# Rotating 96 images by 90 degrees: ten of twelve slabs turned in pairs, and one slab stored in the middle of the loads

## The chip, the cores and the metric

The kernel runs on one core of one Trainium2 chip. The metric is the device time of one execution in microseconds (us), as the median of several runs; lower is better.

## The reference

```python
def setup_inputs():
    batch, c, h, w = 32, 3, 256, 256
    return {"x": np.random.randn(batch, c, h, w).astype(np.float32)}

def reference(x):
    return np.rot90(x, k=-1, axes=(-2, -1)).astype(np.float32)
```

Each of the 96 planes of 256 x 256 floats is turned clockwise: `out[i, j] = x[255 - j, i]`. Nothing is computed; 25.17 MB are read, permuted and 25.17 MB are written.

## The kernel before

**Slabs.** The 96 planes are cut into twelve slabs of eight planes, 2 MB each. A slab lies in SBUF as 128 partitions of 4096 floats (16 KB). A slab can be laid out in two ways, and the way decides how long the contiguous piece of DRAM is that one partition holds, and so how long a DMA row (one contiguous piece) is:

- "short": the slab is two halves of four planes, and a partition holds 8 image rows (8 KB) of each half. The DRAM rows are 8 KB, all 128 partitions take part.
- "long": a partition holds 16 image rows (16 KB) of one plane. The first four planes sit in the even partitions, the other four in the odd ones. The DRAM rows are 16 KB, and one half of a slab takes 64 partitions.

**Turning.** VectorE's 32 x 32 block transpose with a permuted access pattern does the whole rotation of a slab between two SBUF layouts. It can't go from long to long within one slab: a slab that is loaded long is stored short, and the reverse. Two slabs held side by side in one tile can be turned together from long to long, as one operation in four parts. So there are three forms in `turn`:

- slabs 0, 1 and 2 (`long_st`) are loaded short and stored long, two instructions each;
- slabs 3 to 7 are loaded long and stored short, two instructions each;
- the pairs (8, 9) and (10, 11) (`both`) are loaded long and stored long, four instructions a pair.

**Memory.** All twelve slabs fill SBUF, so each turn writes into the buffer of a slab that was turned before. The first one, slab 0, is turned into PSUM (`turned0`); at the end ScalarE copies it from PSUM into the buffer of slab 11, which is free by then, and it is stored from there. `home` and `pairs` say which buffer a turned slab goes to. The tile for slabs 3 and 7 is one pool tile for two slabs, as those of (8, 9) and (10, 11); the program waits per tile, not per slab.

**Order.** All DMAs are issued by SyncE (SP) on one queue. The order is: all loads (slabs 0, 1, 2, 3, 7, 4, 5, 6, 8 to 11); then the stores of slabs 4, 3, 5, 6, 7 (8 KB rows), 1, 2 (16 KB rows); then the pairs (8, 9) and (10, 11), each after its turn; then slab 0. The first store waits by hand for a piece of the last load: the first half of slab 11 is cut for that into a piece of 14 image rows (`mark`) and one of two. Every DMA uses one of eight completion semaphores in turn, so SP waits before a DMA until the one eight places ahead of it has landed.

**Lines.** L92, L88 and L96 issue the loads, L118 is the transpose, L124, L127 and L130 issue 16 KB row stores (L124: both halves of a slab in one DMA of 2 MB), L132 issues 8 KB row stores, L146 is the copy out of PSUM.

Of the kernel before, what the change touches and what calls it, by code (L numbers as in the profile page):

```python
# [1 line left out]

# [4 lines left out]

@with_exitstack
def kernel(
    ctx: ExitStack,
    tc: tile.TileContext,
    x: bass.AP,
    out: bass.AP,
):

    nc = tc.nc
    fp32 = mybir.dt.float32

    B, C, H, W = x.shape
    P = nc.NUM_PARTITIONS
    RL, RS = 16, 8  # L50
    I = 2
    Q = P * RS // H
    n_slabs = B * C // (Q * I)
    last = n_slabs - 1
    F = RS * W
    long_st = (0, 1, 2)
    both = (8, 10)
    paired = [n + a for n in both for a in range(2)]

    rows_in = x.rearrange("b c h w -> (b c h) w")  # L60
    rows_out = out.rearrange("b c h w -> (b c h) w")

    def short(rows):
        return rows.rearrange("(n i p r) w -> n p i (r w)", i=I, p=P, r=RS)

    def long(rows):
        return rows.rearrange("(n i m r) w -> n i m (r w)", i=I, m=P // I, r=RL)

    ld_short, ld_long, st_short, st_long = short(rows_in), long(rows_in), short(rows_out), long(rows_out)

    units = [None] * n_slabs
    adjacent = [(3, 7), (8, 9), (10, 11)]
    pairs = []
    for us in adjacent + [(u,) for u in range(n_slabs) if all(u not in us for us in adjacent)]:
        pool = ctx.enter_context(tc.tile_pool(name=f"unit{us[0]}", bufs=1))
        held = pool.tile([P, len(us), I * F], fp32, name=f"u{us[0]}")
        for j, u in enumerate(us):
            units[u] = held[:, j]
        pairs.append(held)
    psum = ctx.enter_context(tc.tile_pool(name="psum", bufs=1, space=bass.MemoryType.PSUM))  # L80
    turned0 = psum.tile([P, I * F], fp32, name="turned0")

    def fours(t):
        return t.rearrange("p (i f) -> p i f", i=I)

    for n in (0, 1, 2, 3, 7, 4, 5, 6, *range(8, n_slabs)):
        if n in (1, 2):
            nc.sync.dma_start(out=fours(units[n]), in_=ld_short[n])  # L88
            continue
        for i in range(I):  # L90
            if n in long_st:
                ld = nc.sync.dma_start(out=fours(units[n])[:, i], in_=ld_short[n][:, i])  # L92
            else:
                cuts = (0, 14 * W, RL * W) if (n, i) == (last, 0) else (0, RL * W)
                for f0, f1 in zip(cuts, cuts[1:]):
                    ld = nc.sync.dma_start(out=units[n][i::I, f0:f1], in_=ld_long[n, i][:, f0:f1])  # L96
                    if f1 == 14 * W:
                        mark = ld

    home = [turned0] + units[:last]  # L100

    def turn(n):
        if n in long_st:
            src = fours(units[n]).rearrange("p i (r g c) -> p c r g i", r=RS, c=RL)
            dst = home[n].rearrange("p (c k r) -> p c r k", c=RL, r=RS)[:, :, ::-1, ::-1]
            parts, step = 2, RL // 2
        elif n in paired:
            if n not in both:
                return
            src = pairs[both.index(n) + 1].rearrange("p a (r g c) -> p c r g a", r=RL, c=RL)  # L110
            dst = pairs[both.index(n)].rearrange("p i (c k r) -> p c r k i", c=RL, r=RL)[:, :, ::-1, ::-1, :]
            parts, step = 4, RL // 4
        else:
            src = units[n].rearrange("p (r g c) -> p c r g", r=RL, c=RS)
            dst = fours(home[n]).rearrange("p i (c k r) -> p c r k i", c=RS, r=RL)[:, :, ::-1, ::-1, :]
            parts, step = 2, RS // 2
        for h in range(parts):
            nc.vector.transpose(out=dst[:, h * step : (h + 1) * step], in_=src[:, h * step : (h + 1) * step])  # L118

    def store(n):  # L120
        if n in paired:
            first = n if n in both else n - 1
            if n == first:
                nc.sync.dma_start(out=st_long[n].transpose([1, 0, 2]), in_=pairs[both.index(n)][::I])  # L124
                return
            for i in range(I):
                nc.sync.dma_start(out=st_long[n, i], in_=pairs[both.index(first)][n - first :: I, i])  # L127
        elif n in long_st:
            for i in range(I):
                nc.sync.dma_start(out=st_long[n, i], in_=home[n][i::I])  # L130
        else:
            return nc.sync.dma_start(out=st_short[n], in_=fours(home[n]))  # L132

    for n in range(both[0]):
        turn(n)
    for n in (4, 3, 5, 6, 7, 1, 2):
        st = store(n)
        if n == 4:
            tc.add_manual_dep(st.ins, mark.ins.name, mybir.DependencyInfo(
                mybir.DependencyClass.Sync, mybir.DependencyReason.SCHED_ONLY), reason="stores after loads")  # L140
    for n in range(both[0], n_slabs):
        turn(n)
        store(n)

    for i in range(I):
        nc.scalar.copy(out=fours(units[last])[:, i], in_=fours(turned0)[:, i])  # L146
    home[0] = units[last]
    store(0)


# [1 line left out]
_INS = ['x']  # L152
_OUTS = [((32, 3, 256, 256), 'float32')]


# [23 lines left out]
```

## Time and profile before

| | |
|---|---|
| time, median of 3 runs | 123.2 us (123.16 to 123.3) |
| span of the profiled execution | 121.4 us |
| moved | 25.17 MB read, 25.17 MB written, 414 GB/s over the span |
| busy share of the 16 DMA engines | 98.0% |
| VectorE busy | 90.5 us (75%), 24 instructions |
| ScalarE busy | 4.9 us (4%) |
| DMAs | 23 loads and 17 stores, all on one queue |

The time is taken outside the profile. For the profiled execution only its span is on record, from the first to the last profiled instruction; the median lies 1.8 us above it, for what a launch does before and after. In the page, the row DMA gives the busy share of the DMA engines in 40 slices of the span in tenths, and the row GB/s what they moved in each slice. A mark L118 is line 118 of the kernel. In the list of waits of SP, a name on the left is the line whose instruction waited.

### The profile page before, as it was taken

To read this page: it belongs to the slowest core of one execution; us is meant where nothing else is said; L and a number is where in the kernel's file an instruction comes from. 1 tells how busy PE (TensorE), PEld (TensorE's weight loads), DVE (VectorE), ACT (ScalarE), POOL (GpSimd) and SP (SyncE) were. 2 spreads that over 40 slices of the span, in tenths; PEclk is the share of its full clock that TensorE was granted. 3 is DMA by queue.
4 is the path that set the end of the run, shared out by engine and by line. 5 is a ranking of instruction groups with operands and counts; after the bars stand their busy time and mean duration, and the time that the engine had idled before them with its cause. 6 is when DMAs were issued, how large, how long until landed. Compare 5 with 4: busy or idle time off the path is not lost.

```text
span 121.4 us, 134 instructions
## 1 busy us (share of the span) xinstructions
DVE 90.5 (75%) x24; ACT 4.9 (4%) x3; POOL 0.2 (0%) x4
## 2 busy tenths in 40 slices
DVE  0029999999999999999999999999999960000000
ACT  0000000000000000000040000000000038000000
POOL 0000000000000000000000000000000000000000
DMA  3999999999999999999999999999999999999994
GB/s 84 416 432 424 426 459 432 432 432 426 426 432 426 416 421 432 421 426 450 403 424 426 426 429 429 421 432 424 464 426 432 432 432 432 432 432 432 432 432 178
DMA packets 4800, 50.33 MB, mean 414 GB/s; under 512 B 640, under 2 KB 640, under 8 KB 704
## 3 DMA queue, kind: packets, MB, share of 16 engines
q1 hardware_dynamic: 4800, 50.33, 98.0%
HBM read 25.17 MB, written 25.17 MB: 414 GB/s over the span
## 4 chain that ended last, share of the span: by engine, by line
DVE 55%; issue 17%; DMA 6%; DVEq 3%; ACT 2%; ACTq 1%; SPq 0%
DVE u L118 50%; DVE turned L118 6%; DMA u<-in_x_dram 6%; DVEq L174 3%; ACT u L146 2%; ACTq L174 1%; SPq L92 0%; DVEq L118 0%
## 5 line engine op out<-in xcount | busy, mean ns | idle before, releaser
L118 DVE STREAM_TRANSPOSE u<-u 128x2048 f32<-128x2048 f32 x22 | 83.4, 3861 | 0.3
L118 DVE STREAM_TRANSPOSE turned<-u 128x2048 f32<-128x2048 f32 x2 | 7.1, 3584 | 8.3 <-DMA u<-in_x_dram 8.3
L146 ACT COPY u<-turned 128x2048 f32<-128x2048 f32 x2 | 3.6, 1869 | 35.6 <-DVE u L118 35.6
L146 ACT ACT_TABLE_LOAD x1 | 1.3, 1283 | 62.3 <-DMA u<-in_x_dram 62.3
L163 POOL MEMSET const-uint8-127<- 128x1 uint8 x1 | 0.1, 103 | 0.0
L163 POOL MEMSET const-bfloat16-1.0<- 128x1 bf16 x1 | 0.1, 101 | 0.0
L163 POOL MEMSET const-float32-0.0<- 128x1 f32 x1 | 0.1, 99 | 0.2 <-issue 0.2
L163 POOL MEMSET const-float32-1.0<- 128x1 f32 x1 | 0.1, 99 | 0.0
## 6 DMA issues: line engine op xcount, KB each, us to landing
u<-in_x_dram SPq DMA_DIRECT2D x19, 1024.0 KB, 19.6
out_dram<-u SPq DMA_DIRECT2D x7, 2048.0 KB, 16.3
out_dram<-u SPq DMA_DIRECT2D x10, 1024.0 KB, 18.3
u<-in_x_dram SPq DMA_DIRECT2D x2, 2048.0 KB, 13.7
u<-in_x_dram SPq DMA_DIRECT2D x1, 896.0 KB, 19.3
u<-in_x_dram SPq DMA_DIRECT2D x1, 128.0 KB, 17.2
```

The costliest lines, as they stand in the source:

```text
L118: nc.vector.transpose(out=dst[:, h * step : (h + 1) * step], in_=src[:, h * step : (h + 1) * step])
L146: nc.scalar.copy(out=fours(units[last])[:, i], in_=fours(turned0)[:, i])
L163: nc = _bacc.Bacc("TRN2", target_bir_lowering=False, num_devices=1)
L174: with _tile.TileContext(nc) as tc:
```

## The change

Slabs 2 to 11 are now five pairs, each loaded in 16 KB rows, turned from long to long (four instructions) and stored in 16 KB rows by two DMAs of 2 MB. A pair's turned result goes to the tile of the pair ahead of it. Slab 0 is still loaded in 8 KB rows, turned into PSUM, copied by ScalarE at the end and stored in 16 KB rows; its way out is now the buffer of slab 10. Slab 1 is loaded in 16 KB rows, turned into the buffer of slab 11 (which isn't loaded yet), and stored in 8 KB rows between the loads of slab 9 and slab 10. The load of slab 11 must therefore wait until that store has landed. Slabs 0 and 1 share one tile, as does each pair. The cut in the load of slab 11 and its `mark` are gone; the DMAs keep their written order by `queued`. There are 24 loads and 13 stores.

```diff
-    long_st = (0, 1, 2)
-    both = (8, 10)
-    paired = [n + a for n in both for a in range(2)]
...
+    units = []
+    for k in range(n_slabs // A):
+        pool = ctx.enter_context(tc.tile_pool(name=f"unit{k}", bufs=1))
+        units.append(pool.tile([P, A, F], fp32, name=f"u{k}"))
...
+    def move(out, in_):
+        dma = nc.sync.dma_start(out=out, in_=in_)
+        if queued:
+            tc.add_manual_dep(dma.ins, queued[-1].ins.name, mybir.DependencyInfo(
+                mybir.DependencyClass.NoSync, mybir.DependencyReason.SCHED_ONLY), reason="order of the queue")
+        queued.append(dma)
+
+    def load(n):
         for i in range(I):
...
+            if n == 0:
+                move(out=halves(unit(n))[:, i], in_=ld_short[n][:, i])
             else:
...
-                cuts = (0, 14 * W, RL * W) if (n, i) == (last, 0) else (0, RL * W)
-                for f0, f1 in zip(cuts, cuts[1:]):
-                    ld = nc.sync.dma_start(out=units[n][i::I, f0:f1], in_=ld_long[n, i][:, f0:f1])
-                    if f1 == 14 * W:
-                        mark = ld
+                move(out=unit(n)[i::I], in_=ld_long[n][:, i])
...
+    def cut(dst, src, parts):
+        step = src.shape[1] // parts
         for h in range(parts):
             nc.vector.transpose(out=dst[:, h * step : (h + 1) * step], in_=src[:, h * step : (h + 1) * step])
...
+    def turn_pair(k):
+        cut(units[k - 1].rearrange("p i (c k r) -> p c r k i", c=R, r=R)[:, :, ::-1, ::-1, :],
+            units[k].rearrange("p a (r g c) -> p c r g a", r=R, c=R), 4)
+
+    def store_pair(k):
+        for a in range(A):
+            move(out=st_long[A * k + a], in_=units[k - 1][a::A])
+
+    early = 10
+    for n in range(early):
+        load(n)
+    turn_short_long(unit(0), turned)
+    turn_long_short(unit(1), unit(last))
+    move(out=st_short[1], in_=halves(unit(last)))
+    for n in range(early, n_slabs):
+        load(n)
+    for k in range(1, n_slabs // A):
+        turn_pair(k)
+        store_pair(k)
     for i in range(I):
-        nc.scalar.copy(out=fours(units[last])[:, i], in_=fours(turned0)[:, i])
-    home[0] = units[last]
-    store(0)
+        nc.scalar.copy(out=halves(unit(early))[:, i], in_=halves(turned)[:, i])
+    for i in range(I):
+        move(out=st_long[0][:, i], in_=unit(early)[i::I])
```

More of the change, by code (lines that the diff above doesn't have):

```diff
@@ L49 @@
     P = nc.NUM_PARTITIONS
[L50 to L53, printed above, removed]
+    R, RS, I, A = 16, 8, 2, 2
+    M = P // I
+    F = R * W
+    n_slabs = B * C // (P * R // H)
     last = n_slabs - 1
-    F = RS * W
-    long_st = (0, 1, 2)
-    both = (8, 10)
-    paired = [n + a for n in both for a in range(2)]
     rows_in = x.rearrange("b c h w -> (b c h) w")
@@ L66, in long @@
     def long(rows):
-        return rows.rearrange("(n i m r) w -> n i m (r w)", i=I, m=P // I, r=RL)
+        return rows.rearrange("(n i m r) w -> n m i (r w)", i=I, m=M, r=R)
     ld_short, ld_long, st_short, st_long = short(rows_in), long(rows_in), short(rows_out), long(rows_out)
[L71 to L79, printed above, removed]
+    units = []
@@ L80, with unit, halves @@
+    for k in range(n_slabs // A):
+        pool = ctx.enter_context(tc.tile_pool(name=f"unit{k}", bufs=1))
+        units.append(pool.tile([P, A, F], fp32, name=f"u{k}"))
     psum = ctx.enter_context(tc.tile_pool(name="psum", bufs=1, space=bass.MemoryType.PSUM))
-    turned0 = psum.tile([P, I * F], fp32, name="turned0")
-    def fours(t):
+    turned = psum.tile([P, F], fp32, name="turned")
+    def unit(n):
+        return units[n // A][:, n % A]
+    def halves(t):
         return t.rearrange("p (i f) -> p i f", i=I)
[L86 to L89, printed above, removed]
+    queued = []
@@ L90 @@
+    def move(out, in_):
[5 more added lines that the diff above has]
+    def load(n):
         for i in range(I):
-            if n in long_st:
-                ld = nc.sync.dma_start(out=fours(units[n])[:, i], in_=ld_short[n][:, i])
-            else:
-                cuts = (0, 14 * W, RL * W) if (n, i) == (last, 0) else (0, RL * W)
-                for f0, f1 in zip(cuts, cuts[1:]):
-                    ld = nc.sync.dma_start(out=units[n][i::I, f0:f1], in_=ld_long[n, i][:, f0:f1])
-                    if f1 == 14 * W:
-                        mark = ld
@@ L100 @@
[L100 to L116, printed above, removed]
+            if n == 0:
+                move(out=halves(unit(n))[:, i], in_=ld_short[n][:, i])
+            else:
+                move(out=unit(n)[i::I], in_=ld_long[n][:, i])
@@ L117, in turn @@
+    def cut(dst, src, parts):
+        step = src.shape[1] // parts
         for h in range(parts):
             nc.vector.transpose(out=dst[:, h * step : (h + 1) * step], in_=src[:, h * step : (h + 1) * step])
[L120 to L143, printed above, removed]
+    def turn_short_long(src, dst):
+        cut(dst.rearrange("p (c k r) -> p c r k", c=R, r=RS)[:, :, ::-1, ::-1],
+            halves(src).rearrange("p i (r g c) -> p c r g i", r=RS, c=R), 2)
@@ new lines, in turn_long_short @@
+    def turn_long_short(src, dst):
+        cut(halves(dst).rearrange("p i (c k r) -> p c r k i", c=RS, r=R)[:, :, ::-1, ::-1, :],
+            src.rearrange("p (r g c) -> p c r g", r=R, c=RS), 2)
+    def turn_pair(k):
[4 more added lines that the diff above has]
+            move(out=st_long[A * k + a], in_=units[k - 1][a::A])
```

## The prediction

> **What bounds the kernel now.** I read the page first: busy times, slices, DMA queue.
>
> ```profile
> DVE 90.5 (75%) x24; ACT 4.9 (4%) x3; POOL 0.2 (0%) x4
> ...
> DMA  3999999999999999999999999999999999999994
> GB/s 84 416 432 424 426 459 432 432 432 426 426 432 426 416 421 432 421 426 450 403 424 426 426 429 429 421 432 424 464 426 432 432 432 432 432 432 432 432 432 178
> ...
> q1 hardware_dynamic: 4800, 50.33, 98.0%
> ```
>
> The 16 DMA engines are busy from the first slice to the last; VectorE stops 22 us before the end. The page's chain runs through VectorE (50%), but that is the tool following semaphores: no slice of the DMA row shows a hole that VectorE made. So the time is the bytes at the rate of the DMAs, plus ends. Bytes don't change, so I next asked for the rate in four stretches, each of one kind of row: 8 KB loads, 16 KB loads, 8 KB stores, 16 KB stores.
>
> ```profile
> core 0: us, DVE busy (x) ACT busy (x) POOL busy (x), PEclk, DMA share, GB/s
> 7.40:17.20 9.80, 8.91 (x3) 0.00 (x0) 0.00 (x0) 1.00 1.01 429
> 22.20:56.40 34.20, 34.03 (x10) 0.00 (x0) 0.00 (x0) 1.00 1.01 429
> 61.40:85.90 24.50, 24.40 (x8) 1.28 (x1) 0.00 (x0) 1.00 1.01 429
> 85.90:115.00 29.10, 13.17 (x4) 3.63 (x2) 0.00 (x0) 1.00 1.01 431
> ```
>
> Only the 16 KB stores stand out, by 2 GB/s. At such differences a whole GB/s is too coarse, so I took the third digit from the trace's packet records: the mean start of the sixteen packets (one an engine) that open each slab, and the step from slab to slab. Loads in 8 KB rows: 4.900 and 4.912 us for slabs 1 and 2. Loads in 16 KB rows: 4.894 (mean of seven). The slab with the cut piece: 4.932. Stores in 8 KB rows: 4.900, all five. Stores in 16 KB rows: 4.8625 as one DMA of 2 MB, 4.8685 as two of 1 MB.
>
> Last, the timeline of VectorE and SP, for what must arrive before the DMA engines run dry.
>
> ```profile
> 8.25 7.08 DVE L118 STREAM_TRANSPOSE turned<-u 128x2048 f32<-128x2048 f32 x2 [8.25 <-DMA u<-in_x_dram]
> 59.46 11.13 SPq L132 DMA_DIRECT2D out_dram<-u  x5
> 99.10 0.63 SPq L124 DMA_DIRECT2D out_dram<-u  x1
> 99.10 3.63 ACT L146 COPY u<-turned 128x2048 f32<-128x2048 f32 x2 [35.56 <-DVE u L118]
> ```
>
> ```profile
> 8.17 0.47 SPq L96 DMA_DIRECT2D u<-in_x_dram  x1
> ```
>
> ```profile
> 13.14 0.47 SPq L96 DMA_DIRECT2D u<-in_x_dram  x1
> ```
>
> ```profile
> 15.36 7.82 DVE L118 STREAM_TRANSPOSE u<-u 128x2048 f32<-128x2048 f32 x2
> ```
>
> ```profile
> 62.41 7.78 DVE L118 STREAM_TRANSPOSE u<-u 128x2048 f32<-128x2048 f32 x2
> ```
>
> ```profile
> 70.22 14.41 DVE L118 STREAM_TRANSPOSE u<-u 128x2048 f32<-128x2048 f32 x4
> ```
>
> The two SP lines are DMAs that were held until an earlier one landed: slab 0 at 8.17, slab 1 at 13.14. A single slab costs VectorE 7.8 us, a pair in the four-part form 14.4 (7.2 a slab). The last pair's store was issued at 99.10, its packets are due at 105.3 by the steps: 6.2 us of DMA work were still queued.
>
> **The rows (on the path: every ns counts).** Loads: slabs 1 and 2 go from 4.900 + 4.912 to 2 x 4.894: -0.02 us. The cut piece goes: 4.932 to 4.894, -0.04. Stores: before 5 x 4.900 + 2 x 4.8625 + 5 x 4.8685 = 58.57; after 4.900 (slab 1) + 10 x 4.8625 (the pairs, one DMA a slab) + 4.8685 (slab 0) = 58.39; -0.17. Sum -0.24. Other ends: the rounded rates alone give 4 slabs x 2.097 MB x (1/429 - 1/431) = 0.09 plus the cut's 0.04, so -0.13; the packets' median durations (8 KB 309 ns; 16 KB 614 loading, 611 storing; the cut's 540 + 84) give per engine 96 x 309 against 16 x 614 + 32 x 611, plus 4 x 10, so -0.33. The durations overlap slightly (DMA share 1.01), which flatters the removal; the steps don't. I take -0.26, close to the steps.
>
> A rule of the Trainium skill speaks against part of this: "DMA: Bandwidth & Descriptors", section "Rules for kernel authors", says that two transfers to disjoint halves of the partitions aren't worth it and one 128-partition transfer should be used; slabs 1 and 2 go from the one to the other. The row disagrees: 64-partition loads of 16 KB rows step at 4.894, 128-partition loads of 8 KB rows at 4.900. The page's section "Why small descriptors are slow" gives about 3 cycles a packet on the engine's internal bus; 48 packets fewer an engine at the 850 MHz it states would by my estimate be 0.17 us, beside 0.20 from the rows here (all but the cut). No number below comes from it.
>
> **VectorE starts later (covered).** Slabs 0 and 1 now share a tile, and the compiled program's first transpose waits for all four of their loads. It starts at 13.15 instead of 8.25, and all turns are queued behind it. Against that, twelve slabs need 7.11 (slab 0) + 7.85 (slab 1, single form) + 5 x 14.44 = 87.2 us instead of 90.8. End: 100.3, against 99.1. The turns of the pairs end at 42.5, 57.0, 71.4, 85.9, 100.3. The DMA engines want their stores at (7.46, the first packets of slab 1, + 9 x 4.894 + 4.900 + 2 x 4.894 = 66.2, then 9.725 a pair) 66.2, 75.9, 85.6, 95.4, 105.1. The tightest is the last: issued 4.7 us ahead. How far ahead is needed: at start-up 1.05 us from the first issue (0.73) to the first packet (1.78); the first store of before was issued at 59.46 and its packets followed the loads at 61.26 with no hole, so 1.8 is surely enough. Cover left: 2.9 to 3.7 us; beyond that each us costs one. Nothing is paid.
>
> **Store of slab 1 among the loads (covered, one unknown).** It waits on VectorE until 28.1, and for a semaphore until about 35; its packets are due at 51.5. No loss. The load of slab 11 waits until that store has landed: packets done at 56.4, plus 0.8 from there to the last semaphore (the lag of the 8 KB stores before), 57.2. Queued behind it on SP: the other half of slab 11 and every pair store. In the DMA queue stand the two halves of slab 10, until 61.3: 4.1 us ahead, 1.8 needed, 2.3 over. SP then needs 0.5 to 1.4 us an issue, for stores due from 66.2; the first pair was turned at 42.5. Nothing is paid.
> What the trace lacks is the DMA engines going from stores back to loads. The switch from loads to stores shows nothing (step 4.901 beside 4.900). The dearest thing like it is the cold start, where the first packets took 0.69 to 1.3 us instead of 0.31: 0 to 1.0 us. A gain could only be the overlap of the two kinds, at most the 0.03 by which their steps differ. I take 0, since the load-to-store row is a switch in a full queue, as this one is.
>
> **Slab 0's way out (covered).** ScalarE copies at 100.3 for 3.63 us; the store is issued at 104.0 and is due at 114.8. The two stores of 1 MB at the end, and so the tail, stay.
>
> **Sum.** Span 121.43 - 0.26 = 121.17. The span's distance to the median (123.20 - 121.43 = 1.77) belongs to the launch and stays: 122.94.
>
> **Rivals.**
> *The switch back costs (slower side).* Place: the first packets of slab 10, about 56.4. Price 0 to 1.0 us. It eats the gain at 0.26 and makes the kernel measurably slower from 0.51. For it: the first loads of the run were slow. Against it: there the queue was empty, here it is full, and the other switch is free. At 0.7 the time is 123.64.
> *Rows don't matter.* If the 2 GB/s belong to the late phase (VectorE idle, no loads in flight nearby) and not to the row length, the gain is the cut and little more: 123.1. Against it: the step falls from 4.900 to 4.870 just where the rows change, with VectorE still busy.
> *VectorE becomes the bound.* If the four-part form cost in all phases what the single form costs (7.85 a slab), the five pairs end 6.3 us later, at 106.6; with 1.05 to 1.8 to the first packet the hole is 2.5 to 3.3 us, time 125.8. The form was only seen while storing; but the single form takes the same in both phases (7.82 loading, 7.78 storing).
> *Slab 11's wait opens a hole.* It needs 2.3 us more than read above; 123.5 if the lag were 4 us.
>
> **How the numbers follow.** 0.2% (0.25 us) is about what a measurement of this kernel can tell from no change, and my sum lies on that line. Forecast, DMAs fed throughout: 0.76, with -0.13 to -0.33 and the runs' own scatter (123.16 to 123.30) 122.80 to 123.14; a gain over the line 0.50, under it 0.26. Rows don't matter: 0.06, all within. Switch: 0.12, of it 0.02 within, 0.10 slower. VectorE 0.04 and slab 11's wait 0.02, slower. Together faster 0.50, same 0.34, slower 0.16. The range goes from 122.75 (the durations' end and scatter) to 123.6, taking in the second rival and the cheaper part of the switch; outside remain its dearer part, VectorE's and slab 11's cases.
>
> **What would show it.** Right: the DMA row has no slice under 9 between the ends; the first transpose at about 13.1; the last pair's store issued at about 100.3; 431 GB/s over the stores from 66 on; 3920 packets, the semaphores' 592 among them; slab 11's first load issued at about 57.2. Wrong: a dip near 56 to 62 (switch or slab 11's wait) or near 105 (VectorE late); pair turns over 15.5 us; stores at 429 in spite of the long rows.

## The result and the profile after

The changed kernel takes 123.89 us (median of 5 runs, 123.81 to 124.12) against 123.20 before: 1.0057 of the time, 95% interval 1.0046 to 1.0068. It is 0.69 us slower; the forecast was 0.26 us faster. The profiled execution took 123.81 us with a span of 122.0. Ratios here and below leave out executions more than 1.5% above the fastest of their kernel; that is one of all, the profiled execution of the first experiment.

First the page of the changed kernel, the same lines as were shown of the one before.

```profile
DVE 86.7 (71%) x24; ACT 4.9 (4%) x3; POOL 0.2 (0%) x4
...
DMA  3999999999999999999999999999999999999993
GB/s 97 414 435 430 430 430 430 430 430 430 430 430 430 430 430 430 357 408 465 430 430 414 440 430 440 435 430 430 430 430 435 430 430 430 430 430 430 430 430 129
...
q1 hardware_dynamic: 3920, 50.33, 97.5%
```

The DMA row still shows nines from end to end: the engines never ran dry. But the row under it has a dent: 357 and 408 in the 17th and 18th slices, 48.8 to 54.9 us. The packets there are in flight, only slower; a row of busy shares can't show that. The tool counts a packet's bytes where it starts. Spread over the packets' durations, the 17th slice has 351 and the 18th 423, so the loss is nearly all in the 17th, where the last loads ahead of the store of slab 1 run. The two kernels in the same stretches, the one before first:

```profile
20.00:48.00 28.00, 27.86 (x8) 0.00 (x0) 0.00 (x0) 1.00 1.00 427
46.50:51.40 4.90, 4.87 (x3) 0.00 (x0) 0.00 (x0) 1.00 1.01 428
51.70:56.60 4.90, 4.87 (x2) 0.00 (x0) 0.00 (x0) 1.00 0.99 423
66.60:115.20 48.60, 32.40 (x9) 3.63 (x2) 0.00 (x0) 1.00 1.01 431
```

```profile
20.00:48.00 28.00, 27.93 (x9) 0.00 (x0) 0.00 (x0) 1.00 1.01 430
46.50:51.40 4.90, 4.90 (x2) 0.00 (x0) 0.00 (x0) 1.00 1.02 391
51.70:56.60 4.90, 4.90 (x2) 0.00 (x0) 0.00 (x0) 1.00 0.97 411
66.60:115.20 48.60, 33.38 (x10) 3.63 (x2) 0.00 (x0) 1.00 1.01 431
```

The last column is GB/s. In the second stretch, which ends just before the first packets of slab 1's store (51.72 us), the changed kernel is at 391 where the kernel before has 428. The packet records say how: from 49.5 to 51.7 us 31 of the last 48 load packets of 16 KB took 0.71 to 1.24 us where 0.61 is usual. From 53 us on there is no loss any more: the way back to loads, at 57 us, cost nothing.

The timeline after shows the rest on time:

```profile
13.16 7.08 DVE L73 STREAM_TRANSPOSE turned<-u 128x2048 f32<-128x2048 f32 x2 [13.16 <-DMA u<-in_x_dram]
```

```profile
35.15 0.41 SPq L57 DMA_DIRECT2D out_dram<-u  x1
```

```profile
58.07 1.11 SPq L57 DMA_DIRECT2D u<-in_x_dram  x2
```

```profile
100.08 1.92 SPq L57 DMA_DIRECT2D out_dram<-u  x2
```

VectorE started at 13.16 (predicted 13.15), the last pair's store was issued at 100.08 (100.3), slab 11's load at 58.07 (57.2). Slab 11's load had 3.4 us left before its packets were due at 61.5, and none of the covers was used up.

**Where 0.59 us of span come from.** With the same measure as in the prediction (mean start of the sixteen packets that open a slab, one an engine, each right behind the engine's semaphore packet of the DMA before), against the trace of before: loads of slabs 0 to 8 -0.16; the load of slab 9, ahead of the store, 5.48 instead of 4.90, +0.58; slab 1's store 4.90 as before, 0.00; slabs 10 and 11 -0.01; the pair stores 4.862 a slab, -0.18. That is +0.23 at the start of the last slab. (The expectations below have 5.41 for slab 9. The sixteen earliest packets give about that; once the engines are apart, second packets of the engines that are ahead are among them.) From there to the last landing +0.16: every DMA adds 16 increments to its semaphore, and the stretch from the first to the last of them, which was 0.44 us before (and 0.40 here until the second half of slab 9), is 0.76 when slab 9 has landed and 0.84 at the end. The engines have come apart, and the slowest sets the end. From the last landing to the end +0.20; the last is seen in SP's waits after the last store, the kernel before first:

```profile
L174 SPq EVENT_SEMAPHORE  x1: 28/28/28, 120.6 to 120.6; - x1
```

```profile
L131 SPq EVENT_SEMAPHORE  x4: 28/28/28, 121.0 to 121.2; - x4
```

At the end SP waits for the eight semaphores in a fixed order. With 40 DMAs the last one uses the semaphore that is waited for last; with 37 it does not, and three more waits of 65 ns each come after it.

### The profile page after: what moved, and what is told of

It reads as the page before. It is cut to its first block, busy times and chain, and to the rows that moved or that the text cites. A ratio compares the mean times of both kernels' runs of the same rounds, so it can differ in the third digit from the quotient of the medians.

```text
span 122.0 us, 131 instructions
## 1 busy us (share of the span) xinstructions
DVE 86.7 (71%) x24; ACT 4.9 (4%) x3; POOL 0.2 (0%) x4
## 4 chain that ended last, share of the span: by engine, by line
DVE 48%; DMA 15%; issue 13%; DVEq 3%; SPq 3%; ACT 2%; ACTq 1%
DVE u L73 48%; DMA u<-in_x_dram 15%; SPq L57 3%; DVEq L131 3%; ACT u L103 2%; ACTq L131 1%; DVEq L73 0%
## 5 line engine op out<-in xcount | busy, mean ns | idle before, releaser
L73 DVE STREAM_TRANSPOSE u<-u 128x2048 f32<-128x2048 f32 x22 | 79.7, 3705 | 0.2
```

## The experiments

Each ran beside the kernel before on the same chip (medians 123.18 to 123.23 there). Theories: A, a store that is queued long ahead slows the loads in front of it; B, each change of direction of a DMA engine costs in itself; C, the tail depends on the last DMA's semaphore; D, the shape of the store collides with that of the loads; F, the rows' gain as predicted.

**1. Holding the stores back.** First slab 1's, then also the first pair's. `hold` keeps a DMA from being issued until another one has landed.

```diff
     move(out=st_short[1], in_=halves(unit(last)))
+    hold(queued[-1], queued[-3])      # until the first half of slab 9 has landed
...
         store_pair(k)
+        if k == 1:                    # second kernel only
+            hold(queued[-2], queued[-4])
```

> The changed kernel with one wait more: the store of slab 1 is not issued until the first half of slab 9 has landed (about 49.8 us instead of 35.2), some 1.8 us before its packets are due instead of 16. Theory A (a store that stands in the queue long before its turn slows the last loads ahead of it): the long packets at 49.5 to 51.7 us go, the step of slab 9 falls from 5.41 to about 4.90 us, and the time from 123.9 to about 123.3. Theory B (the change of direction itself costs, whenever the store was issued): the step stays near 5.4 and the time at 123.9.

> As the run with slab 1's store held, and the first pair's store held too, until the first half of slab 11 has landed (some 2 us before its packets are due instead of 7). Theory A: the small bump at 65.6 us (step 4.94) goes as well, 0.05 to 0.1 us under the run with one hold, about 123.2. Theory B: 123.9, as the changed kernel.

Measured: 125.39 us (ratio 1.0166, 1.0144 to 1.0188) and 124.06 (1.0066, 1.0046 to 1.0085; single runs from 123.40 to 124.83). One hold, in stretches; the profiled execution was the slowest of its six (126.62 us). The last line is the changed kernel's for the last stretch:

```profile
49.20:51.70 2.50, 2.50 (x2) 0.00 (x0) 0.00 (x0) 1.00 0.91 387
55.50:58.00 2.50, 2.46 (x2) 0.00 (x0) 0.00 (x0) 1.00 1.05 383
64.00:68.00 4.00, 4.00 (x2) 1.11 (x1) 0.00 (x0) 1.00 0.96 315
```

```profile
64.00:68.00 4.00, 4.00 (x3) 0.00 (x0) 0.00 (x0) 1.00 1.01 422
```

What A says of the loads ahead of the store holds, in both traces: the step of slab 9 falls to 4.89 us, and no packet there is long (the 387 is the counting by starts; spread over the durations it is 428). But the loss then comes on the way back to loads: with one hold slab 1's store takes 5.18 and slab 10 5.10, with two holds 5.15 and 4.99. With one hold it comes once more at the last change (315 at 64 to 68, slab 11 6.01), and the engines end 2.8 us apart; for that there is only this one trace, of the slowest execution. Neither theory foresaw it. The other five executions (124.64 to 125.76) are slower than the changed kernel too; where their time goes was not seen.

The two holds have a fault of their own. The first half of slab 11 had landed on all engines only at 65.74 us, the pair store was issued at 65.81, and the engines had begun to run out of loads at 66.15:

```profile
66.00:67.25 1.25, 1.25 (x1) 0.00 (x0) 0.00 (x0) 1.00 0.35 144
```

This hole costs 0.9 us in the profiled execution (slab 2's store 5.80 instead of 4.90; time 124.83); the median lies 0.83 us above before. So these two runs do not show that holding can't help: beside the hole, the 0.34 us on the way back are the largest loss in this trace. A hold that ends a little earlier was not run.

**2. The kernel before without its hold.**

```diff
-        if n == 4:
-            tc.add_manual_dep(st.ins, mark.ins.name, ...)
```

> The kernel before without the hold of its first store by hand: the store is issued at about 47.5 us instead of 59.5, some 14 us before its packets are due; the loads and stores are the same, and nothing goes back from stores to loads. Theory A: the last loads before 61 us get long packets, 0.4 to 0.6 us slower, about 123.7. Theory B: no difference, 123.2.

123.52 us, ratio 1.0024 (1.0015 to 1.0033): +0.29, less than A said, clearly more than B. The last load step is 5.11 where it was 4.93, and 19 load packets from 59 to 62 us are long. So even the one change to stores that the kernel before has is free only because its store is issued late.

**3. The place of the store.** Behind the loads instead of among them; then the same with 40 DMAs.

```diff
-    move(out=st_short[1], in_=halves(unit(last)))
...
         turn_pair(k)
+        if k == 1:
+            move(out=st_short[1], in_=halves(unit(1)))
+            hold(queued[-1], queued[-3])
         store_pair(k)
```

> The changed kernel with the 2 MB store in 8 KB rows moved from between the loads to behind them, held until the first half of slab 11 has landed; it takes its data from the first tile (what it writes is not slab 1, since that buffer is loaded over by then). Bytes, rows and number of DMAs are those of the changed kernel; only the two extra changes of direction are gone. Theory A+B (what the change costs lies in the changes of direction among the loads): no long packets at 49 to 57 us, last landing at 120.3, and with the tail of 1.0 us for 37 DMAs 123.1 (the prediction's 122.94 plus 0.2). Rival (the pairs' rows or the late VectorE cost): stays at 123.9.

> As the run with the store behind the loads (the same data left out), and three pair stores issued as two DMAs of 1 MB, so that there are 40 DMAs. Theory C (the place of the last DMA among the eight semaphores sets the tail): 0.2 us under the run with 37 DMAs, 122.9. Rival: 0.02 us slower for three more DMAs, 123.1.

123.37 us, 1.0015 (1.0007 to 1.0024), and 123.22 us, 1.0002 (0.9992 to 1.0012). About 0.5 of the 0.69 us go with the place of the store, 0.15 with the three DMAs more. The rate where the dent was, from the first of these:

```profile
46.50:51.40 4.90, 4.90 (x2) 0.00 (x0) 0.00 (x0) 1.00 1.01 431
51.70:56.60 4.90, 4.90 (x2) 0.00 (x0) 0.00 (x0) 1.00 1.01 428
```

They lie 0.27 and 0.32 us above what was expected: no gain from the rows is left. (Both store other bytes than the right ones for slab 1, as many and in the same rows.) Their single runs lie 0.6 and 0.75 us apart (122.99 to 123.62, 122.78 to 123.53), those of the kernel before beside them 0.2.

**4. The store among the loads, added to the kernel before.**

```diff
-    for n in (0, 1, 2, 3, 7, 4, 5, 6, *range(8, n_slabs)):   # all loads, then turns and stores
...
+    for n in (0, 1, 2, 3, 7, 4, 5, 6, 8, 9):
+        load(n)
+    for n in range(4):
+        turn(n)
+    store(3)
+    for n in (10, 11):
+        load(n)
```

> The kernel before with one thing changed: the store of slab 3 (turned by 39 us) is issued between the loads of slabs 9 and 10; rows, forms, hold and DMAs stay. Theory A+B: 0.6 to 1.0 us slower, 123.8 to 124.2, with long packets about 50 us or at the way back to loads about 56. Rival (it is the rows, the pairs or the later VectorE of the change that cost): 123.2.

124.00 us, ratio 1.0066 (1.0052 to 1.0080): +0.8. This is the part of the change that costs, by itself, with nothing of the pairs. Its dent is in the same place, and its ten long packets of 50 to 52 us (0.84 us and more) are loads ahead of the store:

```profile
GB/s 89 430 430 430 414 443 430 430 430 430 430 430 430 430 430 430 365 427 454 419 427 412 427 430 427 427 430 430 449 435 430 430 430 425 435 430 425 419 430 161
```

**5. More changes of direction.** The store in two halves at two places; the store in 16 KB rows; the store issued on ScalarE's queue beside the loads, as early as it can be and held until slab 7 has landed.

```diff
-    move(out=st_short[1], in_=halves(unit(last)))
+    move(out=st_short[1][:, 0], in_=halves(unit(last))[:, 0])     # e10: ahead of load(9)
+    move(out=st_short[1][:, 1], in_=halves(unit(last))[:, 1])     # e10: behind it
...
+    for i in range(I):                                            # e7
+        move(out=st_long[1][:, i], in_=unit(last)[i::I])
...
+    nc.scalar.dma_start(out=st_short[1], in_=halves(unit(last)))  # e9; e13 holds it until slab 7 has landed
```

> The changed kernel with the store of slab 1 cut in its two halves of 1 MB, one between the loads of slabs 8 and 9 and one between those of 9 and 10: the same bytes and rows, four changes of direction among the loads instead of two. Theory A+B: the cost of the store among the loads (0.5 to 0.8 us) comes twice, 124.4 to 124.7. Rival (the cost goes with the bytes stored among the loads): 123.9.

> The changed kernel with the store among the loads cut in two DMAs of 64 partitions and 16 KB rows, as the loads around it have them (the bytes go to the right slab in a wrong order). Theory D (the cost comes from engines that serve different partitions side by side, because the store has another shape than the loads): the long packets go, 123.3. Theory B (any change of direction costs): still 123.6 to 124.2.

> The changed kernel with one thing changed: the store of slab 1 is issued by ScalarE on its own queue as soon as the slab is turned (about 28 us), so that the DMA engines serve it beside the loads, one packet of each in turn, instead of between them. Theory B (each change of direction of a DMA engine costs): some 16 changes an engine instead of two, so far slower than the changed kernel, over 125. Rival (the cost is one of two phases meeting, and a mix of both costs nothing or gains by using both directions): 123.2 to 123.4.

> As the run with slab 1's store on ScalarE's queue, but held until slab 7 has landed (about 42.4 us), so that its place among the eight semaphores lies behind the loads of slabs 0 to 9 and no load but slab 11's waits for it. Theory B (each change of direction of an engine costs alike): sixteen changes an engine instead of two, over 125.5 even without a hole in the queue. Rival (most of the 127.9 was the hole that the loads' wait for the store's semaphore left about 40 to 42 us, and a mixed stretch runs at about 393 GB/s instead of 430, 8 us of it costing 0.7 us): 123.8 to 124.3.

Two halves: 124.74 us, 1.0137 (1.0109 to 1.0166), by the medians +1.5 against before and +0.85 against the changed kernel for the same bytes. Long packets lie ahead of each half, 29 of them at 44 to 47 us and 8 at 51. The cost goes with how often a store stands among the loads, not with how much it stores.

Same shape as the loads: 124.71 us, 1.0131 (1.0115 to 1.0147). D falls: alike in rows and partitions, the store costs even more (slab 9 5.34 us, slab 10 5.24, engines 1.57 us apart at the end).

On ScalarE's queue: 127.88 us, 1.0384 (1.0370 to 1.0398), and held 126.52 us, 1.0262 (1.0243 to 1.0281). Both times look like B, and neither is: each kernel waits where it was not meant to. In the first, SP's loads wait for the semaphore that the store uses, 22 us of waiting (the list of SP's waits, its line in us, times, longest):

```profile
SPq L57 <- DMA out_dram<-u: 22.1, 1, 22.1
```

and the DMA engines run dry at 40 to 42 us (66 GB/s in that stretch). In the second, the store beside the loads takes until 59.6 us, so that slab 11's load is issued only at 60.2, 1.6 us before the loads ahead of it end. Slab 11 takes 6.96 us. Of the 2.1 us too many the engines stand idle for some 0.24; the rest is long packets ahead of the first pair's store. What the second does show lies before that. Its store's packets run from 46.2 to 59.6 us, one by one among those of the loads:

```profile
44.00:46.00 2.00, 2.00 (x2) 0.00 (x0) 0.00 (x0) 1.00 1.07 360
46.00:48.00 2.00, 2.00 (x2) 0.00 (x0) 0.00 (x0) 1.00 0.93 377
48.00:50.00 2.00, 2.00 (x2) 0.00 (x0) 0.00 (x0) 1.00 1.01 430
50.00:52.00 2.00, 2.00 (x1) 0.00 (x0) 0.00 (x0) 1.00 1.03 438
52.00:54.00 2.00, 2.00 (x2) 0.00 (x0) 0.00 (x0) 1.00 0.97 414
54.00:56.00 2.00, 2.00 (x1) 0.00 (x0) 0.00 (x0) 1.00 1.04 442
```

From 48 us on the mix runs at 430 GB/s, as loads alone do, though every engine goes back and forth with each packet. The loss is at the onset, 44 to 48 us: 0.55 us against a steady 430 GB/s. It begins at 44.5, 2 us after the store was issued (42.52) and ahead of its first packet. So B falls as it was put: going back and forth costs the engines nothing that shows in this stretch. The long packets lie ahead of the first packets of a store, also here. That is so in every trace of a kernel whose store stands among the loads and was issued early, and there are none ahead of a store that was held and came just in time (the kernel before, the store behind the loads). How much is lost varies: 0.2 to 0.9 us ahead of a store among the loads, 0.06 ahead of the changed kernel's first pair store, which was issued 7 us ahead, and 1.1 at the same place in the first kernel with ScalarE's queue, issued 14 us ahead.

**6. The rows alone.** The kernel before with all stores in 16 KB rows and 48 DMAs.

```diff
-            return nc.sync.dma_start(out=st_short[n], in_=fours(home[n]))
+            sts = [nc.sync.dma_start(out=st_long[n, i], in_=home[n][i::I]) for i in range(I)]
+            return sts[0]
```

> The kernel before with nothing changed but the rows of the stores of slabs 3 to 7, now 16 KB (two DMAs of 64 partitions a slab; the bytes of these slabs go out in a wrong order), and with 48 DMAs, so that the last one still uses the last semaphore. Theory F (the rows' gain as predicted, 4.900 to 4.8685 us a slab): 0.16 us faster, 123.05. Rival (the rate of the 16 KB stores is that of how the engines stand to each other, not of the rows): 123.2, with steps of 4.86 to 4.90 in the stores.

123.22 us, ratio 1.0000 (0.9991 to 1.0009): no gain, and the predicted 0.16 us lies outside the interval. In the profiled execution the rows do what was read before, 431 GB/s where the 8 KB rows of the kernel before had 428 (its line first):

```profile
62.00:85.00 23.00, 22.90 (x8) 1.28 (x1) 0.00 (x0) 1.00 1.01 428
```

```profile
62.00:85.00 23.00, 22.90 (x8) 1.28 (x1) 0.00 (x0) 1.00 1.01 431
```

But that execution, at 122.96, is the fastest of the eleven; the others go up to 123.32. The rate of 16 KB stores is not the same in every execution: 4.86 to 4.87 us a slab in this profile and in that of the changed kernel, 4.89 to 4.92 in that of the kernel with the late store and 40 DMAs, no better than the 8 KB rows of before. Loads in 16 KB rows vary as well: slabs 1 to 4 of the changed kernel step at 4.87, its slabs 6 to 8 at 4.89.

**7. The tail alone, and 40 DMAs in the changed kernel.**

```diff
-            for i in range(I):
-                nc.sync.dma_start(out=st_long[n, i], in_=pairs[both.index(first)][n - first :: I, i])
+            nc.sync.dma_start(out=st_long[n].transpose([1, 0, 2]), in_=pairs[both.index(first)][n - first :: I])
```

> The kernel before with the second slab of each late pair stored by one DMA of 2 MB instead of two of 1 MB: 38 DMAs instead of 40, all else as it was. Theory C (the tail depends on which of the eight semaphores the last DMA uses): 0.1 to 0.2 us slower, 123.3 to 123.4, all of it between the last landing and the end. Rival: 123.2, or 0.01 less for two DMAs fewer.

> The changed kernel with three of the pair stores issued as two DMAs of 1 MB, so that there are 40 DMAs instead of 37 and the last one uses the last of the eight semaphores that SP waits for in turn at the end. Theory C (the four waits that SP still has to go through after the last landing cost 0.2 us of tail): the stretch from the last landing to the end falls from 1.0 to 0.8 us, time about 123.7. Rival: the tail does not depend on it, and the three more DMAs make it 123.9.

38 DMAs: 123.33 us, 1.0010 (1.0001 to 1.0019), +0.13 us. In its trace three waits follow the last landing instead of one,

```profile
L173 SPq EVENT_SEMAPHORE  x3: 28/28/28, 120.7 to 120.8; - x3
```

and the stretch from the last landing to the end is 0.94 us, 0.81 with 40 DMAs and 1.01 with 37. The changed kernel with 40 DMAs has its 0.81 there, yet takes 123.96 (1.0058, 1.0043 to 1.0073), where 123.7 was expected: its runs, 123.54 to 124.30, are too far apart to show 0.2 us, and in the profiled one slab 9 takes 5.77. In the pair of section 3 the difference was 0.15.

## Why the prediction was wrong

- **The step that failed** is the term for the store of slab 1 among the loads, put at nothing: "its packets are due at 51.5. No loss", with "The switch from loads to stores shows nothing (step 4.901 beside 4.900)" behind it. The row was real, but its store had been held back by hand to 1.8 us before its turn; without the hold the same change costs 0.29 us. The store of slab 1 was issued 16 us ahead, and the change to it cost 0.58 us, all on the loads ahead of it. The text counted the lead as cover against a hole and gave it no price.
- **The unknown that the text did name**, the way from stores back to loads ("I take 0"), came out at 0: slab 1's store took 4.90 and slab 10 4.87. So the first rival had the size right by luck (up to 1.0 us; a store among the loads measured +0.8 when added to the kernel before), but its place and its cause, the first packets of slab 10, were wrong; the sign to look for, a dip near 56 to 62, came at 49 to 52.
- **"The two stores of 1 MB at the end, and so the tail, stay"** was wrong by 0.20 us after the last landing: the DMAs stayed, their semaphore did not. The number of DMAs was in the listing of both kernels, 40 and 37, and wasn't followed to the end. Another 0.16 us lie ahead of the last landing, because the engines had come apart; the text had no term for that.
- **The rows' -0.26** were a term read right from one execution and mis-sized for the median. The profile after has the stores' part (-0.18); its loads gain 0.16 up to slab 8, where the sum had 0.02, because 16 KB rows ran at 4.87 us a slab in slabs 1 to 4 and not at 4.89. That part is luck. By itself on the kernel before it measured 0.00 (-0.11 to +0.11), and in the changed kernel without the inner store and with 40 DMAs +0.02. The second rival, rows don't matter, was right on that. (The 7.46 us from which the due times start is 7.57 in the trace; that moves them by 0.1 us and no conclusion.)
- **VectorE's later start, slab 11's wait, slab 0's way out** were costed at nothing and cost nothing; their times came within 0.9 us of those predicted. The faster pair form took back most of what the later start lost: VectorE began 4.9 us later than before, and the last pair's store was issued 1.0 us later (100.08 against 99.10), 0.2 us earlier than worked out.
- The upper end of the range, 123.6, had room for a switch of 0.66 us but not for the tail's 0.20 on top of it.

What stays open: why the loads are slowed ahead of a store that was issued early, and what sets the size; and why a late issue helps the kernel before (0.29 us) while in the changed one a loss then comes on the way back to loads. Excluded are a difference in shape between store and loads and the back and forth of single engines.

## What to carry to other kernels

On a queue that is always full, loads first and stores after was worth more here than the rows: each store among the loads cost 0.5 to 0.9 us, whether of 1 or 2 MB, and in 16 KB rows, or with this one store held back, the time was longer still. A free change of direction in a profile is evidence only for a store that is issued as late as that one. A gain of 0.2% read from the rates of one execution needs a second execution before it is called a gain.

## What the runs showed of the hardware that was not expected

- Loads and stores mixed packet by packet from two queues run at 430 GB/s once they are under way, as each does alone; the loss (360 to 377 GB/s for 4 us) is at the onset and begins before the store's first packet.
- The sixteen DMA engines mostly keep the distance they get: 0.44 us from the first to the last increment all through the kernel before, 0.84 after one store among the loads, 1.6 with its two halves apart, 2.8 in the worst run, with steps of 4.862 us behind it all the same. With two holds it shrank again, from 1.9 to 0.86 us over the hole and on to 0.46 by the end, with steps of 4.90.
- A busy share of 9 tenths or more hides a loss of a tenth in bytes (391 GB/s instead of 428 at a DMA share of 1.02); GB/s beside it shows it.
- Each wait of SP that is left after the last landing costs 65 ns, so the number of DMAs modulo the eight semaphores moves the tail: 0.81 us with 40, 0.94 with 38, 1.01 with 37.
